# Expert matrices: output copies on ScalarE, another order of the low parts, raw weights as halves of their rows

## The chip, the cores and the metric

The kernel runs on one core of a Trainium2 chip. The metric is the device time of one execution in microseconds, as the median of several. The engines are TensorE (PE, its weight loads shown as PEld), VectorE (DVE), ScalarE (ACT), GpSimd (POOL) and SyncE (SP, which issues most transfers).

## The reference

One step of a two-layer diffusion backbone on 128 context tokens and 1024 latent tokens, width 1024, in float32. Layer 0 mixes tokens by a gated linear recurrence, layer 1 by a chunked spatial gate. Behind each mixer stands an expert-choice mixture of experts, which is where the change lies:

```
def _ec_moe(x, router, w_gate, w_up, w_down):
    cap = EC_FACTOR * (bsz * t) // N_EXPERTS        # 128 latent tokens, 16 context tokens per expert
    aff = jax.nn.softmax(xf @ router, axis=-1)
    g, idx = lax.top_k(aff.T, cap)
    xs = xf[idx]
    hh = silu(einsum('ecd,edf->ecf', xs, w_gate)) * einsum('ecd,edf->ecf', xs, w_up)
    out = einsum('ecf,efd->ecd', hh, w_down) * g[..., None]
    y = zeros_like(xf).at[idx.reshape(-1)].add(out.reshape(-1, d))
```

There are 16 experts in each of the two layers, each with three matrices of 1024x1024 float32, 4 MB each.

## The kernel before

**Numbers in two parts.** A float32 weight is scaled and written as the sum of two float16 numbers: `whi` (the rounded value, an ACT copy) and `wlo` (the rest, a DVE subtraction). The tokens are split likewise into `Sh` and `Sl`, the hidden activations into `Hh` and `Hl`. A product is three float16 matmuls: whi·Sh, whi·Sl, wlo·Sh.

**Steps.** An expert is worked off in 12 steps, which the code calls pairs, because each covers two blocks of 128 output columns. In step n, `i = n % 12`: i = 0 to 3 are the gate matrix, 4 to 7 the up matrix, 8 to 11 the down matrix. A step is 2 blocks x 8 slices of the inner dimension x 3 products = 48 matmuls of 128x144 (128 latent and 16 context tokens). They go into a tile `mm` of PSUM, one bank for each block, of which there are two, so that step n + 2 needs what step n left there to have been read. The program issues each step as 36 matmuls (inner slices 0 to 5), then other work, then the 12 matmuls of slices 6 and 7.

**What reads `mm` (`evacuate`, L1722 ff.).** Gate steps: ACT applies SiLU into `sg` (L1733). Up steps: DVE multiplies with `sg` into `t` (L1738); `hidden` then makes `Hh` (ACT, L1743; for the last of the four steps DVE, L1745) and `Hl` (DVE, L1746). Down steps: DVE writes the 128 latent columns into `oT` (L1752) and the 16 context columns into `pt` (L1753), each times a gain. Step 8 reads all of H, so `hidden` of step 7 stands right ahead of it.

**Around the steps.** An expert's tokens are gathered by an indirect transfer (`xg`), turned by 8 PE transposes in step 8 of the expert before (`xgT`, L1661), scaled by ACT into `tmp` (8 activations of 128x128, L1674) and split into `Sh` (ACT, L1685) and `Sl` (DVE, L1686), in two halves. A finished expert's `oT` is turned back by 8 transposes in step 1 of the next (`oTT`), scaled by ACT (`o`, L1765) and added to the result in DRAM by an indirect transfer.

**Weights ahead.** A raw half matrix of 2 MB (`raw`) is loaded by one transfer on SP (L1617) into one of five buffers: all 1024 rows, 512 of the 1024 columns, so 2 KB per row. `split_hi` and `split_lo` make the parts of a later step piece by piece, two pieces a step, each of 128 partitions x 1024 elements, into 12 buffers of `whi` and 12 of `wlo`. A piece is one block of 128 columns with all 8 inner slices. When the last piece of a raw half has its `wlo`, the buffer is given to the load of five halves later. Two tables, `HIS` and `LOS`, say for each of the 12 steps how many pieces are issued at three places: behind the 36 matmuls and ahead of `hidden`, behind `hidden`, and behind the last 12 matmuls. The high parts run about five steps ahead of the matmuls, the low parts four. The first four steps' pieces of a layer are loaded and split during the mixer by the class `First`.

Each engine works its queue strictly in order, so these tables decide what stands ahead of what on ACT and DVE:

```
            rest = evacuate(n - 1) if n > 0 else None
            if i == 8:
                rest()
                rest = None
            matmuls(n, range(6))
            ahead(n, 0)
            if rest:
                rest()
            ahead(n, 1)
```

**The last expert of layer 1** has the final norm beside its steps: ACT squares the finished rows, POOL multiplies them by the gain, DVE works out the factor 1/rms in small operations (L103 to L113).

Of the kernel before, what the change touches and what calls it, by code (L numbers as in the profile page):

```python
# [23 lines left out]
P = 128  # L24
KD = D // P
# [14 lines left out]
UP, DOWN = 2.0 ** 8, 2.0 ** -4  # L40
# [3 lines left out]
def tile_trunk(  # L44
# [10 lines left out]
    V, A, PE, G, SP = nc.vector, nc.scalar, nc.tensor, nc.gpsimd, nc.sync  # L55
# [34 lines left out]
    half = cp.tile([P, 1], F32, name="half")  # L90
# [140 lines left out]
    def rows(ch):  # L231
        return slice(ch * P, (ch + 1) * P)
# [147 lines left out]
    class First:  # L380


        N = 8

        def __init__(self, l, carry, room):
# [2 lines left out]

        def load(self, c):
            if c < self.N:  # L390
                self.raw[c] = self.room(f"first{self.l}_{c}").rearrange("p (k n) -> p k n", k=KD)
                SP.dma_start(self.raw[c], self.src[:, :, rows(c)])

        def split(self, c):
            if c < self.N:
                p = [self.carry.tile([P, KD, P], F16, tag=f"w{s}", name=f"w{s}{self.l}_f{c}", bufs=12) for s in ("hi", "lo")]
                split_up(self.raw.pop(c), *p)
                self.parts.append(p)

# [10 lines left out]
    class Route:  # L410
# [140 lines left out]
                A.activation(d[:, i], ps[:, P * i:P * (i + 1)], AF.Identity, bias=self.big[:, 1, 4 * q + i:4 * q + i + 1])  # L551

        def halve(self):
            self.xh, self.xl = (self.room(n, [P, KD, P], F32R) for n in ("xph", "xpl"))
            A.copy(self.xh, self.post.xnp.rearrange("t (k p) -> t k p", p=P))

        def halve_rest(self, h):
# [10 lines left out]
        def slots_prompt(self):  # L568

            pr = self.ps.tile([P, NE], F32, tag="misc", name=f"rank{self.l}", bufs=1)  # L570
            for e in range(NE):
                PE.matmul(pr[:, e:e + 1], self.gt[:, e], ones[:, 0:1], start=True, stop=True)
            rk = sm.tile([P, NE], F32, tag="rk", name=f"rk{self.l}")
            V.tensor_scalar_add(rk, pr, 1.0)
            self.oh = self.room("oh", [P, NE, CAPP], F32R)
            V.tensor_tensor(self.oh, rk[:, :, None].to_broadcast([P, NE, CAPP]),
                            slot1[:, None, 0:CAPP].to_broadcast([P, NE, CAPP]), op=OP.is_equal)

# [18 lines left out]
        def weights(self):  # L597

            self.og = self.room("og", [P, NE, CAPP], F32)
            V.tensor_tensor(self.og, self.oh.bitcast(F32), self.af[:, 8, :, None].to_broadcast([P, NE, CAPP]), op=OP.mult)  # L600
            self.ogT = self.ps.tile([P, 4, P], F32, tag="tr", name=f"ogT{self.l}")
            for h in range(2):
                PE.transpose(self.ogT[:, h], self.og[:, 8 * h:8 * h + 8].rearrange("p e s -> p (e s)"), ident)
# [991 lines left out]
    def moe(l, post, route, firsts, carry, close):  # L1595
        es = ExitStack()
        posm, info, pt, ohg, idxs, gs = route.posm, route.info, route.pt, route.ohg, route.idxs, route.gs
        wp = pool_of(es, f"moew{l}")
# [4 lines left out]
        g2 = cp.tile([P, 2, KD], F32, name=f"g2_{l}")  # L1603
        G.tensor_scalar(g2, modc[l, 5], 1.0 / (UP * DOWN), None, op0=OP.mult)

        raws, ws, xg, evac = {}, {}, {}, {}
        S, H, sg, oT, oTT, tmps = {}, {}, {}, {}, {}, {}
        NPAIR = 12 * NE

        def load(m):  # L1610

            if m >= 6 * NE:
                return
            e, which, half = m // 6, m % 6 // 2, m % 2
            t = raws[m] = wp.tile([P, KD, FF // 2], F32, tag="raw", name=f"raw{l}_{m}", bufs=5)
            w = (moe_w_gate, moe_w_up, moe_w_down)[which]
            SP.dma_start(t, w[l, e].rearrange("(k p) f -> p k f", p=P)[:, :, 512 * half:512 * (half + 1)])  # L1617

        def block(n, b):
            m, j = divmod(n, 2)  # L1620
            return raws[m][:, :, P * (2 * j + b):P * (2 * j + b + 1)]

        def split_hi(n, b):
            if n < NPAIR:
                hi = carry.tile([P, KD, P], F16, tag="whi", name=f"whi{l}_{n}_{b}", bufs=12)
                A.activation(hi, block(n, b), AF.Copy, scale=UP)  # L1626
                ws[n, b] = [hi]

        def split_lo(n, b):
            if n < NPAIR:  # L1630
                lo = carry.tile([P, KD, P], F16, tag="wlo", name=f"wlo{l}_{n}_{b}", bufs=12)
                V.scalar_tensor_tensor(lo, block(n, b), UP, ws[n, b][0], op0=OP.mult, op1=OP.subtract)  # L1632
                ws[n, b].append(lo)
                if n % 2 == 1 and b == 1:
                    raws.pop(n // 2)
                    load(n // 2 + 5)


        def slots_a(e):
# [24 lines left out]
        def tokens_b(e, ps, h):  # L1664

            if h == 0:
                tmps[e] = mp.tile([P, KD, 144], F32, tag="tmp", name=f"tmp{l}_{e}")
                V.tensor_copy(tmps[e][:, :, P:], pt[:, :, CAPP * e:CAPP * (e + 1)])
            for k in range(4 * h, 4 * h + 4):
                o = tmps[e][:, k, 0:P]  # L1670
                if e == 0 and h == 0:
                    V.tensor_scalar(o, ps[h][:, k], s2[:, 1, k:k + 1], sh2[:, 1, k:k + 1], op0=OP.mult, op1=OP.add)
                else:
                    A.activation(o, ps[h][:, k - 4 * h], AF.Identity, bias=sh2[:, 1, k:k + 1], scale=s2[:, 1, k:k + 1])  # L1674
# [14 lines left out]
        AHEAD = 4  # L1689
# [16 lines left out]
        tp = pool_of(es, f"moet{l}")  # L1706
        for h in range(2):
            tokens_c(0, h)
        split_hi(AHEAD, 0)


        def matmuls(n, ks):
            e, i = divmod(n, 12)
            hi, lo = S[e] if i < 8 else H[e]
            if n not in evac:
                evac[n] = psw.tile([P, 2, 512], F32, tag="mm", name=f"mm{l}_{n}", bufs=2)
            ps = evac[n]
            for b in range(2):
                wh, wl = ws[n, b]
                for k in ks:  # L1720
                    for i, (w, x) in enumerate(((wh, hi), (wh, lo), (wl, hi))):
                        PE.matmul(ps[:, b, 0:144], w[:, k], x[:, k], start=(k == 0 and i == 0), stop=(k == KD - 1 and i == 2))  # L1722

        def evacuate(n):
            e, i = divmod(n, 12)
            kind, j = divmod(i, 4)
            ps = evac.pop(n)
            js = slice(2 * j, 2 * j + 2)
            ps = ps[:, :, 0:144]
            if kind == 0:  # L1730
                if j == 0:
                    sg[e] = mp.tile([P, KD, 144], F32, tag="tmp", name=f"sg{l}_{e}")
                A.activation(sg[e][:, js], ps, AF.Silu, scale=1.0 / UP)  # L1733
            elif kind == 1:
                if j == 0:
                    H[e] = [tp.tile([P, KD, 144], F16, tag=f"H{x}", name=f"H{x}{l}_{e}") for x in "hl"]
                t = tp.tile([P, 2, 144], F32, tag="mmt", name=f"t{l}_{n}", bufs=2)
                V.scalar_tensor_tensor(t, ps, DOWN / UP, sg[e][:, js], op0=OP.mult, op1=OP.mult)  # L1738

                def hidden():  # L1740
                    hi, lo = (x[:, js] for x in H[e])
# [13 lines left out]

# [267 lines left out]
```

## Time and profile before

| | |
|---|---|
| median of 3 runs | 2587.98 us (2587.79 to 2589.66) |
| the profiled execution, its span | 2586.94 us, 2584.8 us |
| busy: PE, DVE, ACT, POOL | 2432.3 us (94%), 1909.0 (74%), 1641.5 (64%), 257.6 (10%) |
| mean granted PE clock | 0.974 |
| moved by the transfers | 647.19 MB, 250 GB/s in the mean |
| experts of layer 0; of layer 1 | about 569 to 1200 us; 1924 to 2562 us |

Busy time of an engine is a union of its instructions; neighbours may overlap by some tens of nanoseconds, so the distance from one start to the next is what an instruction costs its queue. "Idle before" is the time for which an engine stood still ahead of an instruction, with the one that released it. Matmuls are pipelined: one of 128x144 is listed with 226 ns, but the next starts much sooner.

### The profile page before, as it was taken

The page shows a single profiled execution, that of the slowest core. Times are in us where ns is not written, and L with a number is a line of the kernel's source. Part 1 is how long each engine was busy: PE and PEld are TensorE (multiplying, and loading weights), DVE is VectorE, ACT ScalarE, POOL GpSimd, SP SyncE. Part 2 cuts the span into 40 slices and gives each one's busy share as a digit, 9 for nine tenths or more (in the row PEclk, how much of TensorE's full clock was granted, in tenths as well). Part 3 has the DMA queues.
Part 4 walks back from the last instruction along what each step waited for, and adds up shares of the span by engine and source line. Part 5 has one row for each costly group of instructions (what it writes and reads, how often), then busy time and mean ns, then how long its engine had stood idle before and what let it go on. Part 6 is the DMA issues. An engine that isn't in the chain of part 4 may idle for free. (4 is left out here: it accounts for less than half of the span.)

```text
span 2584.8 us, 60548 instructions
## 1 busy us (share of the span) xinstructions
PE 2432.3 (94%) x26054; PEld 1850.6 (72%) x26054; DVE 1909.0 (74%) x2790; ACT 1641.5 (64%) x2336; POOL 257.6 (10%) x307
## 2 busy tenths in 40 slices
PE   6999989969999999998999999999969999999996
PEld 4455554459999999997434455534459999999995
DVE  6888895479999999996622333445679999999997
ACT  5877883448777777885623333434448778777874
POOL 1011101100000000001201100100100000000003
PEclk9999999979999999998999999999979999999998
DMA  9466216459999999994544533457559999999994
GB/s 321 166 206 206 76 64 200 157 205 339 342 355 354 345 330 360 342 354 136 178 151 163 175 114 111 153 190 233 191 212 342 346 350 355 347 329 360 341 350 164
DMA packets 330236, 647.19 MB, mean 250 GB/s; under 512 B 15555, under 2 KB 69367, under 8 KB 329967
## 3 DMA queue, kind: packets, MB, share of 16 engines
q1 hardware_dynamic: 306352, 568.49, 62.0%
q0 software_dynamic: 21136, 74.67, 9.2%
q8 instruction: 204, 3.34, 0.5%
q10 hardware_dynamic: 2478, 0.16, 0.1%
q14 instruction: 66, 0.53, 0.1%
HBM read 576.59 MB, written 66.68 MB: 249 GB/s over the span
## 5 line engine op out<-in xcount | busy, mean ns | idle before, releaser
L1722 PEld LDWEIGHTS <-whi 128*128 128x128 f16 x12032 | 966.8, 98 | 28.0 <-issue 22.2
L1632 DVE SCALAR_TENSOR_TENSOR wlo<-raw,whi 128x1024 f16<-128x1024 f32 x752 | 885.5, 1221 | 25.5 <-ACT whi L1626 25.5
L1626 ACT ACTIVATE whi<-raw 128x1024 f16<-128x1024 f32 x752 | 756.0, 1060 | 53.3 <-PE mm L1722 49.8
L1722 PE MATMUL mm<-Sh,whi 128*128 128x144 f16 x3968 | 747.6, 226 | 0.8 <-DVE t L1738 0.8
L1722 PE MATMUL mm<-Sh,wlo 128*128 128x144 f16 x3968 | 747.6, 226 | 0.0
L1722 PE MATMUL mm<-Sl,whi 128*128 128x144 f16 x3968 | 747.6, 226 | 0.0
L1722 PEld LDWEIGHTS <-wlo 128*128 128x128 f16 x6016 | 589.2, 98 | 13.9 <-issue 13.7
L1722 PE MATMUL mm<-Hh,whi 128*128 128x144 f16 x2048 | 390.2, 227 | 20.3 <-DVE Hh L1745 15.4
L1722 PE MATMUL mm<-Hl,whi 128*128 128x144 f16 x2048 | 389.1, 227 | 9.8 <-DVE Hl L1746 9.8
L1722 PE MATMUL mm<-Hh,wlo 128*128 128x144 f16 x2048 | 389.1, 227 | 0.0
L1327 PE MATMUL uv<-sgw,h_hi 128*128 128x512 f16 x576 | 219.6, 381 | 0.0
L1328 PE MATMUL uv<-sgw,h_hi 128*128 128x512 f16 x576 | 219.3, 381 | 0.0
L1329 PE MATMUL uv<-sgw,h_lo 128*128 128x512 f16 x576 | 219.1, 380 | 0.0
L1333 ACT ACTIVATE uvo<-uv 128x512 f32<-128x512 f32 x72 | 43.0, 597 | 198.5 <-PE uv L1329 198.5
L896 PE MATMUL pj<-hn_hi,wh 128*128 128x386 f16 x480 | 157.8, 329 | 1.9 <-ACT hn_hi L116 1.9
L897 PE MATMUL pj<-hn_lo,wh 128*128 128x386 f16 x480 | 157.5, 328 | 0.2
L898 PE MATMUL pj<-hn_hi,wl 128*128 128x386 f16 x480 | 157.5, 328 | 0.0
L1766 POOL DMA_INDIRECT x_d<-o,idx x31 | 55.8, 1799 | 965.1 <-ACT o L1765 933.8
L1440 DVE SCALAR_TENSOR_TENSOR uvo<-sv,bs,uvo 128x256 f32<-128x256 f32 x72 | 31.5, 480 | 140.4 <-PE sv L1437 140.4
L1346 DVE TENSOR_TENSOR uvo<-uvo,gain 128x512 f32<-128x512 f32 x36 | 24.9, 691 | 134.1 <-ACT uv L1345 134.1
L1674 ACT ACTIVATE tmp<-xgT,modc,ns 128x128 f32<-128x128 f32 x248 | 90.5, 468 | 45.2 <-DVE t L1738 40.2
L1327 PEld LDWEIGHTS <-h_hi 128*128 128x128 f16 x576 | 56.5, 98 | 69.4 <-issue 10.1
(413 smaller groups left out, 3892.0 us busy)
## 6 DMA issues: line engine op xcount, KB each, us to landing
raw<-in_moe_w_up_dram SPq DMA_DIRECT2D x64, 2048.0 KB
raw<-in_moe_w_down_dram SPq DMA_DIRECT2D x64, 2048.0 KB
raw<-in_moe_w_gate_dram SPq DMA_DIRECT2D x60, 2048.0 KB
wm<-in_w_mod_dram SPq DMA_DIRECT2D x96, 512.0 KB
m<-mt_d SPq DMA_DIRECT2D x72, 256.0 KB
sgr<-in_sg_w_in_dram SPq DMA_DIRECT2D x32, 512.0 KB
win<-in_lru_w_in_dram SPq DMA_DIRECT2D x20, 512.0 KB
v_d<-uvo POOLq DMA_DIRECT2D x36, 256.0 KB, 2.4
```

Of the source, the lines that this page charges most:

```text
L896: PE.matmul(ps[:, i, 0:WP], wh[:, k], hi[k][:, cs], start=(k == 0), stop=False)
L897: PE.matmul(ps[:, i, 0:WP], wh[:, k], lo[k][:, cs], start=False, stop=False)
L898: PE.matmul(ps[:, i, 0:WP], wl[:, k], hi[k][:, cs], start=False, stop=(k == KD - 1))
L1327: PE.matmul(ps, hi[:, k, cs], th[:, k % 4], start=(k == 0), stop=False)
L1328: PE.matmul(ps, hi[:, k, cs], tl[:, k % 4], start=False, stop=False)
L1329: PE.matmul(ps, lo[:, k, cs], th[:, k % 4], start=False, stop=(k == KD - 1))
L1333: A.activation(o, ps, AF.Gelu_apprx_tanh, scale=1.0 / UP)
L1626: A.activation(hi, block(n, b), AF.Copy, scale=UP)
L1632: V.scalar_tensor_tensor(lo, block(n, b), UP, ws[n, b][0], op0=OP.mult, op1=OP.subtract)
L1674: A.activation(o, ps[h][:, k - 4 * h], AF.Identity, bias=sh2[:, 1, k:k + 1], scale=s2[:, 1, k:k + 1])
L1722: PE.matmul(ps[:, b, 0:144], w[:, k], x[:, k], start=(k == 0 and i == 0), stop=(k == KD - 1 and i == 2))
L1766: G.indirect_dma_start(out=x_d[0:NS, :], out_offset=bass.IndirectOffsetOnAxis(ap=idxs[:, e:e + 1], axis=0), in_=o, in_offset=None, compute ...
```

## The change

1. **Outputs.** `oT` of a down step is written by ACT in two activations of 128x128 (a copy with a factor per partition) instead of one DVE product of 128x256. DVE keeps `pt`. The copy of `pt` into `tmp` goes from DVE to ACT as well, but for a layer's first expert.
2. **Order of the parts.** New `HIS` and `LOS`, 24 pieces per expert as before. In steps 5 to 7 one low part stands ahead of `hidden`, and in step 7 it is the only one. The second half of the tokens' scaling moves from step 9 to step 10, its split from 10 to 11. Two high parts instead of one are issued ahead of the loop.
3. **Raw weights as halves of their rows.** A raw half is now 512 of the 1024 rows with all columns, 4 KB per row, and a piece is 4 inner slices of both blocks (128 x 4 x 256). Each step takes one piece from each of two raw halves, so a pair of halves serves four steps and the two are given up one right after the other. `First` loads and splits the same way (1 KB instead of 512 B per row).
4. **Buffers.** 14 of `whi` and 13 of `wlo`. `xph`, `xpl` and `oh` of the routing stage become float16, so that its 16 matmuls of 128x256 per layer are float16 with weight loads of their own.

DVE in expert 6 of layer 0 before, from `t` of step 6 (`t_78`) to the first reads of a down step; `sg`, `Hh`, `Hl`, `raw` as above, `waits` names the engine or transfer queue waited for:

```order
L1738 SCALAR_TENSOR_TENSOR t_78_10399<-mm_78_10338,sg_6_9999 128x288 [waits PE_49]
L1746 TENSOR_TENSOR Hl_6_10274<-t_78_10399,Hh_6_10273 128x288 [waits Activation_49]
L1632 SCALAR_TENSOR_TENSOR wlo_84_0_10442<-raw_42_9936,whi_84_0_10393 128x1024 [waits DMAHW0_49]
L1632 SCALAR_TENSOR_TENSOR wlo_84_1_10458<-raw_42_9936,whi_84_1_10438 128x1024
L1738 SCALAR_TENSOR_TENSOR t_79_10460<-mm_79_10401,sg_6_9999 128x288 [waits PE_49]
L1745 CAST Hh_6_10273<-t_79_10460 128x288 [waits DVE_49]
L1746 TENSOR_TENSOR Hl_6_10274<-t_79_10460,Hh_6_10273 128x288 [waits DVE_49]
L1632 SCALAR_TENSOR_TENSOR wlo_85_0_10503<-raw_42_9936,whi_85_0_10456 128x1024 [waits Activation_49]
L1668 COPY tmp_7_10526<-pt_4674 128x8x16
L1752 TENSOR_TENSOR oT_6_10532<-mm_80_10464,g_0_4845 128x256 [waits PE_49]
```

The same place in the changed kernel:

```order
L1742 SCALAR_TENSOR_TENSOR t_78_10425<-mm_78_10362,sg_6_10023 128x288 [waits PE_49]
L1634 SCALAR_TENSOR_TENSOR wlo_84_0_10466<-raw_42_9961,whi_84_0_10399 128x1024 [waits DMAHW0_49]
L1750 TENSOR_TENSOR Hl_6_10298<-t_78_10425,Hh_6_10297 128x288 [waits Activation_49]
L1742 SCALAR_TENSOR_TENSOR t_79_10484<-mm_79_10427,sg_6_10023 128x288 [waits PE_49]
L1749 CAST Hh_6_10297<-t_79_10484 128x288 [waits DVE_49]
L1750 TENSOR_TENSOR Hl_6_10298<-t_79_10484,Hh_6_10297 128x288 [waits DVE_49]
L1634 SCALAR_TENSOR_TENSOR wlo_84_1_10527<-raw_43_10156,whi_84_1_10423 128x1024 [waits DMAHW1_49]
L1634 SCALAR_TENSOR_TENSOR wlo_85_0_10552<-raw_42_9961,whi_85_0_10464 128x1024
L1759 TENSOR_TENSOR pt_4674<-mm_80_10488,g_0_4845 128x2x16 [waits PE_49,Activation_49]
```

Of the two low parts that stood between `Hl` of step 6 and `t_79` of step 7 one stands ahead of that `Hl` and the other behind the three operations of step 7. `oT` is gone from DVE, and `pt` waits for Activation.

ACT in the same expert before, from the last high part of step 7 through steps 8 to 11:

```order
L1626 ACTIVATE whi_85_1_10501<-raw_42_9936 128x1024 [waits PE_49,Activation_49]
L1674 ACTIVATE tmp_7_10526<-xgT_7_10505,modc_3_1390,ns_2_3377 128x128 [waits DVE_49,PE_49,Activation_49]
L1674 ACTIVATE tmp_7_10526<-xgT_7_10505,modc_3_1390,ns_2_3377 128x128 x7
L1626 ACTIVATE whi_86_0_10588<-raw_43_10044 128x1024 [waits DMAHW1_49,PE_49]
L1685 CAST Sh_7_10594<-tmp_7_10526 128x576 [waits DVE_49,Activation_49]
L1626 ACTIVATE whi_86_1_10637<-raw_43_10044 128x1024 [waits PE_49]
L1685 CAST Sh_7_10594<-tmp_7_10526 128x576 [waits Activation_49]
L1626 ACTIVATE whi_87_0_10655<-raw_43_10044 128x1024 [waits PE_49]
L1626 ACTIVATE whi_87_1_10698<-raw_43_10044 128x1024 [waits PE_49]
```

ACT in the changed kernel, from the first output copy, ahead of which four `tmp` stand, to the second `Sh`:

```order
L1758 ACTIVATE oT_6_10560<-mm_80_10488,g_0_4845 128x128 [waits PE_49]
L1758 ACTIVATE oT_6_10560<-mm_80_10488,g_0_4845 128x128
L1628 ACTIVATE whi_87_0_10601<-raw_42_9961 128x1024
L1628 ACTIVATE whi_87_1_10617<-raw_43_10156 128x1024
L1688 CAST Sh_7_10621<-tmp_7_10554 128x576 [waits Activation_49]
L1758 ACTIVATE oT_6_10560<-mm_81_10564,g_0_4845 128x128 [waits PE_49]
L1758 ACTIVATE oT_6_10560<-mm_81_10564,g_0_4845 128x128
L1677 ACTIVATE tmp_7_10554<-xgT_7_10529,modc_3_1390,ns_2_3377 128x128 x4
L1628 ACTIVATE whi_88_0_10683<-raw_44_10202 128x1024 [waits DMAHW2_49]
L1758 ACTIVATE oT_6_10560<-mm_82_10628,g_0_4845 128x128 [waits PE_49]
L1758 ACTIVATE oT_6_10560<-mm_82_10628,g_0_4845 128x128
L1688 CAST Sh_7_10621<-tmp_7_10554 128x576 [waits Activation_49]
```

The eight `tmp` and the two `Sh` are drawn apart, and three of an expert's four pairs of `oT` copies stand ahead of the second `Sh`; the fourth follows it after one high part.

The diff, without the float16 lines of the routing stage, whose tiles `xph`, `xpl`, `oh` only change their type, and with one row pair of each table:

```
         def load(self, c):                                   # class First
             if c < self.N:
-                self.raw[c] = self.room(f"first{self.l}_{c}").rearrange("p (k n) -> p k n", k=KD)
-                SP.dma_start(self.raw[c], self.src[:, :, rows(c)])
+                n, h = divmod(c, 2)
+                self.raw[c] = self.room(f"first{self.l}_{c}").rearrange("p (k n) -> p k n", k=4)
+                SP.dma_start(self.raw[c], self.src[:, 4 * h:4 * h + 4, 256 * n:256 * (n + 1)])
...
-            t = raws[m] = wp.tile([P, KD, FF // 2], F32, tag="raw", name=f"raw{l}_{m}", bufs=5)
+            t = raws[m] = wp.tile([P, KD // 2, FF], F32, tag="raw", name=f"raw{l}_{m}", bufs=5)
...
-            SP.dma_start(t, w[l, e].rearrange("(k p) f -> p k f", p=P)[:, :, 512 * half:512 * (half + 1)])
+            SP.dma_start(t, w[l, e].rearrange("(k p) f -> p k f", p=P)[:, 4 * half:4 * half + 4])
-        def block(n, b):
-            m, j = divmod(n, 2)
-            return raws[m][:, :, P * (2 * j + b):P * (2 * j + b + 1)]
+        def block(n, h):
+            return raws[n // 4 * 2 + h][:, :, 256 * (n % 4):256 * (n % 4 + 1)]
...
-                if n % 2 == 1 and b == 1:
-                    raws.pop(n // 2)
-                    load(n // 2 + 5)
+                if n % 4 == 3:
+                    m = n // 4 * 2 + h
+                    raws.pop(m)
+                    load(m + 5)
...
-                V.tensor_copy(tmps[e][:, :, P:], pt[:, :, CAPP * e:CAPP * (e + 1)])
+                (A.copy if e else V.tensor_copy)(tmps[e][:, :, P:], pt[:, :, CAPP * e:CAPP * (e + 1)])
...
-        split_hi(AHEAD, 0)
+        for h in range(2):
+            split_hi(AHEAD, h)
...
             for b in range(2):
-                wh, wl = ws[n, b]
                 for k in ks:
+                    wh, wl = (w[:, k % 4, P * b:P * (b + 1)] for w in ws[n, k // 4])
...
-                V.tensor_tensor(oT[e][:, js], ps[:, :, 0:P], g2[:, 1, js, None].to_broadcast([P, 2, P]), op=OP.mult)
+                for b in range(2):
+                    c = 2 * j + b
+                    A.activation(oT[e][:, c], ps[:, b, 0:P], AF.Copy, scale=g2[:, 1, c:c + 1])
...
-        LOS = ((1, 0, 1), (2, 0, 1), (1, 0, 1), (1, 0, 1), (2, 0, 1), (0, 1, 1), (0, 1, 1), (0, 1, 1), (1, 0, 0), (0, 0, 1), (1, 0, 1), (1, 0, 1))
+        LOS = ((1, 0, 1), (2, 0, 1), (1, 0, 1), (1, 0, 1), (2, 0, 1), (1, 1, 0), (1, 1, 0), (1, 0, 0), (1, 0, 1), (1, 0, 1), (1, 0, 1), (0, 0, 1))
...
-            if more and i == 9:
+            if more and i == 10:
                 tokens_b(e + 1, hold["x"], 1)
-            if more and i == 10:
+            if more and i == 11:
                 tokens_c(e + 1, 1)
```

## Rows read from the trace of the kernel before

**Rows 1.** Windows, layer 0, an expert of layer 1: PE, PEld, DVE, ACT, POOL

```profile
590.00:1165.00 575.00, 562.37 (x8784) 556.84 (x8782) 524.64 (x710) 455.35 (x619) 43.65 (x28) 1.00 0.97 346
...
2037.21:2076.28 39.07, 38.28 (x604) 37.97 (x602) 35.68 (x48) 31.09 (x43) 3.14 (x2) 1.00 0.99 352
```

**Rows 2.** Waits, whole run, layer 0, layer 1: us, times, longest

```profile
PE mm L1722 <- DVE Hh L1745: 15.4, 30, 0.5
...
PE mm L1722 <- DVE Hl L1746: 4.1, 15, 0.3
PE mm L1722 <- DVE t L1738: 0.9, 2, 0.4
...
PE mm L1722 <- DVE Hl L1746: 5.7, 16, 1.7
```

**Rows 3.** Timelines, PE and DVE, at step 8: start, us, instruction, [idle before]

```profile
2031.83 1.04 PE L1661 MATMUL xgT<-ident,xg 128*128 128x128 f32 x8
2033.38 0.22 PE L1722 MATMUL mm<-Hh,whi 128*128 128x144 f16 x1 [0.51 <-DVE Hh L1745]
...
2030.26 2.35 DVE L1632 SCALAR_TENSOR_TENSOR wlo<-raw,whi 128x1024 f16<-128x1024 f32 x2
2032.53 0.45 DVE L1738 SCALAR_TENSOR_TENSOR t<-mm,sg 128x288 f32<-128x288 f32 x1
2033.01 0.31 DVE L1745 CAST Hh<-t 128x288 f16<-128x288 f32 x1
2033.36 0.46 DVE L1746 TENSOR_TENSOR Hl<-t,Hh 128x288 f16<-128x288 f32 x1
```

**Rows 4.** Chain behind that wait: start, us, what

```profile
2033.87 15.10 PE mm L1722 x239
```

**Rows 5.** Groups by line, three experts: count | busy, mean ns | idle

```profile
L1674 ACT ACTIVATE tmp<-xgT,modc,ns 128x128 f32<-128x128 f32 x24 | 8.7, 468 | 4.0 <-DVE t L1738 4.0
...
L1752 DVE TENSOR_TENSOR oT<-mm,g 128x256 f32<-128x256 f32 x12 | 5.0, 419 | 0.0
L1686 DVE TENSOR_TENSOR Sl<-tmp,Sh 128x576 f16<-128x576 f32 x6 | 4.5, 755 | 2.7 <-ACT Sh L1685 2.7
```

**Rows 6.** Timeline of ACT, steps 8 and 9 of that expert

```profile
2033.10 2.91 ACT L1674 ACTIVATE tmp<-xgT,modc,ns 128x128 f32<-128x128 f32 x8 [1.34 <-DVE t L1738]
2035.87 1.09 ACT L1626 ACTIVATE whi<-raw 128x1024 f16<-128x1024 f32 x1
2036.82 0.70 ACT L1685 CAST Sh<-tmp 128x576 f16<-128x576 f32 x1
```

**Rows 7.** DMA, 40 slices of 2030-2050, 1880-1916, 2530-2546; one issue

```profile
GB/s 418 422 397 401 414 418 406 401 401 430 406 401 401 430 365 254 205 295 307 348 406 414 410 410 406 414 393 205 82 0 20 106 160 385 426 406 389 401 426 406
...
GB/s 0 0 46 182 400 405 412 412 403 410 410 412 407 410 405 414 410 410 405 414 407 405 412 410 394 400 407 412 414 410 391 378 57 16 0 0 0 0 0 0
...
GB/s 10 0 0 0 164 20 61 430 399 440 420 410 420 410 420 399 451 410 440 410 451 389 389 410 399 430 430 420 400 420 440 410 430 430 225 20 31 31 0 0
...
2044.40 0.37 SPq L1617 DMA_DIRECT2D raw<-in_moe_w_gate_dram  x1
```

**Rows 8.** Timelines of DVE, ACT, POOL and PE, last expert of layer 1

```profile
2542.37 2.57 DVE L1746 TENSOR_TENSOR Hl<-t,Hh 128x288 f16<-128x288 f32 x1
...
2548.42 2.33 DVE L111 TENSOR_TENSOR rstf<-rsrf 128x4 f32<-128x4 f32 x1 [1.23 <-POOL rsrf L105]
...
2541.03 1.05 ACT L1833 ACTIVATE fin<-fin 128x1024 f32<-128x1024 f32 x1
2542.21 1.06 ACT L1833 ACTIVATE fin<-fin 128x1024 f32<-128x1024 f32 x1
...
2542.26 4.90 POOL L1840 TENSOR_TENSOR fin<-fin,gain 128x1024 f32<-128x1024 f32 x2 [9.75 <-ACT fin L1833]
...
2548.37 9.27 POOL L1840 TENSOR_TENSOR fin<-fin,gain 128x1024 f32<-128x1024 f32 x4
...
2555.84 0.30 PE L1722 MATMUL mm<-Hh,whi 128*128 128x144 f16 x1 [4.00 <-DVE pt L1753]
```

More of the change, by code (lines that the diff above doesn't have):

```diff
@@ L390, in load @@
             if c < self.N:
-                self.raw[c] = self.room(f"first{self.l}_{c}").rearrange("p (k n) -> p k n", k=KD)
-                SP.dma_start(self.raw[c], self.src[:, :, rows(c)])
+                n, h = divmod(c, 2)
+                self.raw[c] = self.room(f"first{self.l}_{c}").rearrange("p (k n) -> p k n", k=4)
+                SP.dma_start(self.raw[c], self.src[:, 4 * h:4 * h + 4, 256 * n:256 * (n + 1)])
         def split(self, c):
             if c < self.N:
-                p = [self.carry.tile([P, KD, P], F16, tag=f"w{s}", name=f"w{s}{self.l}_f{c}", bufs=12) for s in ("hi", "lo")]
+                p = [self.carry.tile([P, 4, 256], F16, tag=f"w{s}", name=f"w{s}{self.l}_f{c}", bufs=dict(hi=14, lo=13)[s]) for s in ("hi", "lo")]
                 split_up(self.raw.pop(c), *p)
@@ L553, in halve @@
         def halve(self):
-            self.xh, self.xl = (self.room(n, [P, KD, P], F32R) for n in ("xph", "xpl"))
+            self.xh, self.xl = (self.room(n, [P, KD, P], F16) for n in ("xph", "xpl"))
             A.copy(self.xh, self.post.xnp.rearrange("t (k p) -> t k p", p=P))
@@ L574, in slots_prompt @@
             V.tensor_scalar_add(rk, pr, 1.0)
-            self.oh = self.room("oh", [P, NE, CAPP], F32R)
+            self.oh = self.room("oh", [P, NE, CAPP], F16)
             V.tensor_tensor(self.oh, rk[:, :, None].to_broadcast([P, NE, CAPP]),
@@ L599, in weights @@
             self.og = self.room("og", [P, NE, CAPP], F32)
-            V.tensor_tensor(self.og, self.oh.bitcast(F32), self.af[:, 8, :, None].to_broadcast([P, NE, CAPP]), op=OP.mult)
+            V.tensor_tensor(self.og, self.oh, self.af[:, 8, :, None].to_broadcast([P, NE, CAPP]), op=OP.mult)
             self.ogT = self.ps.tile([P, 4, P], F32, tag="tr", name=f"ogT{self.l}")
@@ L1614, in load, with split_hi, split_lo @@
             e, which, half = m // 6, m % 6 // 2, m % 2
-            t = raws[m] = wp.tile([P, KD, FF // 2], F32, tag="raw", name=f"raw{l}_{m}", bufs=5)
+            t = raws[m] = wp.tile([P, KD // 2, FF], F32, tag="raw", name=f"raw{l}_{m}", bufs=5)
             w = (moe_w_gate, moe_w_up, moe_w_down)[which]
-            SP.dma_start(t, w[l, e].rearrange("(k p) f -> p k f", p=P)[:, :, 512 * half:512 * (half + 1)])
-        def block(n, b):
-            m, j = divmod(n, 2)
-            return raws[m][:, :, P * (2 * j + b):P * (2 * j + b + 1)]
-        def split_hi(n, b):
+            SP.dma_start(t, w[l, e].rearrange("(k p) f -> p k f", p=P)[:, 4 * half:4 * half + 4])
+        def block(n, h):
+            return raws[n // 4 * 2 + h][:, :, 256 * (n % 4):256 * (n % 4 + 1)]
+        def split_hi(n, h):
             if n < NPAIR:
[L1625 to L1629, printed above, removed]
+                hi = carry.tile([P, 4, 256], F16, tag="whi", name=f"whi{l}_{n}_{h}", bufs=14)
+                A.activation(hi, block(n, h), AF.Copy, scale=UP)
+                ws[n, h] = [hi]
+        def split_lo(n, h):
             if n < NPAIR:
-                lo = carry.tile([P, KD, P], F16, tag="wlo", name=f"wlo{l}_{n}_{b}", bufs=12)
-                V.scalar_tensor_tensor(lo, block(n, b), UP, ws[n, b][0], op0=OP.mult, op1=OP.subtract)
-                ws[n, b].append(lo)
-                if n % 2 == 1 and b == 1:
-                    raws.pop(n // 2)
-                    load(n // 2 + 5)
+                lo = carry.tile([P, 4, 256], F16, tag="wlo", name=f"wlo{l}_{n}_{h}", bufs=13)
+                V.scalar_tensor_tensor(lo, block(n, h), UP, ws[n, h][0], op0=OP.mult, op1=OP.subtract)
+                ws[n, h].append(lo)
+                if n % 4 == 3:
+                    m = n // 4 * 2 + h
+                    raws.pop(m)
+                    load(m + 5)
         def slots_a(e):
@@ L1718, in matmuls @@
             for b in range(2):
-                wh, wl = ws[n, b]
                 for k in ks:
+                    wh, wl = (w[:, k % 4, P * b:P * (b + 1)] for w in ws[n, k // 4])
                     for i, (w, x) in enumerate(((wh, hi), (wh, lo), (wl, hi))):
-                        PE.matmul(ps[:, b, 0:144], w[:, k], x[:, k], start=(k == 0 and i == 0), stop=(k == KD - 1 and i == 2))
+                        PE.matmul(ps[:, b, 0:144], w, x[:, k], start=(k == 0 and i == 0), stop=(k == KD - 1 and i == 2))
         def evacuate(n):
@@ L1893, in moe @@
         hold = {}
-        his = iter([(m, b) for m in range(AHEAD, NPAIR + 1) for b in range(2)][1:])
+        his = iter([(m, b) for m in range(AHEAD + 1, NPAIR + 1) for b in range(2)])
         los = iter([(m, b) for m in range(AHEAD, NPAIR) for b in range(2)])
@@ L1902, in ahead @@
                 split_lo(m, b)
-        HIS = ((2, 0, 1), (1, 0, 1), (1, 0, 1), (1, 0, 1), (2, 0, 1), (1, 0, 1), (1, 0, 1), (1, 0, 1), (1, 0, 0), (0, 0, 1), (1, 0, 1), (1, 0, 1))
-        LOS = ((1, 0, 1), (2, 0, 1), (1, 0, 1), (1, 0, 1), (2, 0, 1), (0, 1, 1), (0, 1, 1), (0, 1, 1), (1, 0, 0), (0, 0, 1), (1, 0, 1), (1, 0, 1))
+        HIS = ((1, 0, 1), (1, 0, 1), (2, 0, 1), (1, 0, 2), (1, 0, 1), (1, 0, 1), (1, 0, 1), (1, 0, 1), (1, 0, 1), (1, 0, 1), (0, 0, 1), (0, 0, 1))
+        LOS = ((1, 0, 1), (2, 0, 1), (1, 0, 1), (1, 0, 1), (2, 0, 1), (1, 1, 0), (1, 1, 0), (1, 0, 0), (1, 0, 1), (1, 0, 1), (1, 0, 1), (0, 0, 1))
         for n in range(NPAIR):
```

## The prediction

> **What bounds the kernel now.** I looked first at the windows by stage. In the experts PE is busy 562 of 575 us at full granted clock, and a middle expert takes 39.07 us, 38.28 of them PE, 35.68 DVE, 31.09 ACT [rows 1]. So the expert stages, 1250 of 2585 us (32 experts at 39.07), are PE's own pace plus a little waiting, and the change can win at most that waiting. The waits of PE come next: 30 times 0.51 us for `Hh` and 30 times about 0.27 us for `Hl` [rows 2], once per expert, always in step 8. Nowhere in the experts does PE wait for a transfer or for ACT in the steady state.
>
> The timelines show how this wait arises [rows 3]. PE has finished the 36 matmuls of step 8 that it can do, turns the next tokens (until 2032.87), and then stands until 2033.38, because DVE spent 2030.26 to 2032.5 on two low parts and began `t` of step 7 at 2032.53. Behind the wait the matmuls follow each other every (15.10 - 0.23)/238 = 62.5 ns [rows 4], so a step is 48 x 62.5 = 3.0 us. Step 7 therefore ended about 2032.87 - 1.04 - 36 x 0.0625 = 2029.6, and `t` was 2.9 us late behind queued work, not for want of data.
>
> **The change part by part.**
>
> *Low parts in another order.* In step 7 one low part stands ahead of the last `Hl` and none between it and `t` of step 7. From the end of step 6 DVE now has `t` (0.45), one low part (2.35/2 = 1.18), `Hl` (0.46), together 2.1 us inside a step of 3.0, so `t` of step 7 can start as soon as its matmuls are through (their 0.23 us). From there `Hh` starts 0.48 later, `Hl` 0.35 after that and takes 0.46: 1.5 us after the end of step 7 all of H is there. PE needs it after 2.25 + 1.04 = 3.3 us. Even a DVE that is 1.2 us late from the steps before still makes it. The wait goes: 15.4 + 4.1 + (5.7 - 1.7) = 23.5 us, where the 1.7 is the longest one, in the very last expert, which has another cause (below). What was hidden there, the displaced low parts, moves to steps 8 to 10, where `oT` no longer takes DVE 4 x 0.42 = 1.7 us per expert [rows 5]. DVE falls from 35.7 to about 34.0 us.
>
> *Outputs on ACT.* Not seen before; nearest is `tmp`, also ACT from PSUM, 128x128, with one operand more. It costs (2035.87 - 2033.10)/8 = 0.346 us from start to start, 0.468 alone [rows 5, 6]. I take 0.346, because the copies come in twos and between other ACT work; an even cheaper one would change nothing, since it is hidden. Eight are 2.8 us per expert, 31.1 + 2.8 + 0.3 (the small copy of `pt`) = 34.2 of 38.3 us. The tight place is the second `Sh`, now behind three pairs of copies. From the end of step 8: 0.23 for the matmuls, six copies 2.08, three high parts at 0.95 2.85, four `tmp` 1.38, two `Sh` at 0.70 1.40, together 7.94; `Sl` (0.76 and a little) is done at 8.8. PE reads this half after three steps and 12 matmuls, 9.75 us. The margin of 1.0 us holds for copies up to 0.346 + 1.0/6 = 0.51 us, above the 0.468 of a lone one. So I cost this edit at nothing.
>
> The Trainium skill speaks against the move: "ScalarE: Activation LUTs", Rules for kernel authors, gives multiplications to VectorE, which it calls faster per element. The row agrees in size (0.69 us on ACT against 0.42 on DVE); by the rule the move loses 1.1 us of engine time per expert, by the row of PE's waits none of it is on the path.
>
> *`pt` behind `oT`.* `pt` on DVE now waits for both ACT copies of its step, which the order shows as a wait for Activation. Queued behind it are low parts and `Sl`. It adds at most 0.23 + 0.69 + 0.12 = 1.04 us four times, less where DVE comes late itself. 34.0 + 4 x 1.04 = 38.2, just inside the 38.3 that PE needs. The low parts run four steps ahead, so single waits are absorbed: nothing, with little to spare.
>
> *Raw halves of rows.* PE waits for no transfer, so a faster one gains nothing; the question is a loss. An expert moves 39.07 x 0.352 = 13.7 MB. Rows of 2 KB run at about 408 GB/s in the long stretch of the second line of [rows 7], rows of 4 KB (the final norm's loads) at about 417 in the third. The first line has one gap per expert: six slices of 0.5 us that move 573 in place of 6 x 410, 2.3 us lost. Shortening the expert by 0.78 leaves 1.5. A load takes about 7 us from its issue: the one at 2044.40 is at full rate in the slice from 2046.0, and 2 MB at 410 are 5.1. The tightest of the new halves is given up late in step 2 and first read late in step 6, 12 us later; 7 and 2.6 for an expert's gather and scatter (1.05 MB) leave 2.4. Cost nothing. The strides of the raw halves are the only other difference for ACT and DVE, and PE's weights stay rows of 128 in a row.
>
> *Float16 routing tiles, three more buffers, one high part more ahead of the loop.* Matmuls of the same columns; the 16 new weight loads per layer hide as those of 128x144 do at 62.5 ns. If none hid, at most 16 x 0.15, my allowance, on layer 0's entry: 0 to +2.4, taken 0.
>
> *The ends.* Layer 0's last step: the second ACT copy ends 0.346 + 0.468 = 0.8 behind its start against 0.42, so +0.4. Layer 1's last expert: POOL's gain products block small DVE work; `Hl` took 2.57 us and a 128x4 operation 2.33, one POOL product (9.27/4) [rows 8]. `pt` of step 9 stands behind three such, and PE waited 4.00 for it. Squares 1 to 3 now stand behind the output copies of step 8, which wait for that step, while before ACT squared from 2541.03 on every 1.18 us. Measured from the end of step 6: step 8 ends at about 6.5, copies 0.7, three squares 3.5, the factor's first steps 1.5, three blocked operations 7.0, `pt` 0.2, so PE goes on at about 19.4. Before, step 6 ended at 2544.94 (the end of `Hl`) - 1.7 - 2.25 - 3.0 = 2538.0, and PE went on at 2555.84, 17.8 later. That is +1.6, and +0.4 for the last copies. The 1.7 us wait for `Hl` shrinks inside this sum. Bounds: -1.7 if the squares do not matter, +5 if two more POOL products get in front.
>
> The expert that carries the prompt products has two further waits for `t` per layer (0.9 in layer 0 [rows 2]); its queue is as full as before, so I leave them: 0, bounds -1.7 and +1.
>
> Sum: -23.5 + 0.4 + 2.0 = -21.1 us on an execution of 2586.94 (span 2584.8). The median, 2587.98, stands 1.0 above that, and I take it as base: **2566.9 us**.
>
> **Rivals.**
>
> *A. ACT too late for the next tokens.* Lone durations throughout give 0.23 + 6 x 0.468 + 3 x 1.09 + 4 x 0.468 + 1.40 + 0.8 = 10.4 against 9.75: a new wait of 0.65 in step 0 and a gain of 0.13 x 30 = 4, less 2.4 at the ends, 2586. Half of that wait gives 2576; I put 2581. For it: ACT is the engine that gains work, in strict order. Against: its rows overlap by 0.1 us wherever two stand together.
>
> *B. DVE held by `pt`, slower.* If the copies often stand behind a high part (0.95), `pt` waits 1.5 us on average: 34.0 + 6.0 = 40.0 us per expert, +0.93 x 30 + 2.4, 2618. It decides from a mean wait of 1.07 us (PE starts to wait), and loses from 1.27 on. For it: DVE's 34.0 leave little. Against: ACT reaches step 8 idle, and where ACT is late DVE has low parts of its own in front.
>
> *C. Transfers bind.* The DMA share is 0.99, and if 351 GB/s is what they can do, the expert stays at 39.07 and the ends cost: 2590, no change. Against: stretches above 400 and the gap. The Trainium skill ("DMA: Bandwidth & Descriptors", Where 436 GB/s comes from) has a rule that speaks for C: from HBM to SBUF the HBM side, about 358 GB/s, binds. By it 13.7 MB take 38.4 us, the gain stops at 30 x 0.67 = 20 less 2.4, and the time is 2570; the stretch at 408 disagrees, and I follow the row.
>
> **How the numbers follow.** Forecast 0.74, own range 2561 (all lower bounds) to 2574 (the upper bounds of ends and weight loads); A 0.10, B 0.10, C 0.06. Under 0.2% (5 us) this kernel can't be told from no change. Faster: 0.74 and most of A, 0.80; same: rest of A and C, 0.10; slower: B, 0.10. The range 2559 to 2585 takes the forecast and nearly all of A; B and most of C stay out.
>
> **What would show it.** Right: no PE wait for `Hh` or `Hl` in step 8, an expert at 38.3 us, ACT busy near 34, DVE near 34 with a new wait of `pt` for ACT of 2 to 3 us per expert, output copies near 0.47 us listed. Layer 1's last expert somewhat longer than before. Wrong: PE waiting for `Sl` in step 0 (A), for `pt` in steps 10 and 11 or a `wlo` anywhere (B), ACT waiting for `raw` (C).

## The result and the profile after

| | before | changed |
|---|---|---|
| median, same chip | 2588.07 us | 2553.89 us (2553.10 to 2557.19) |
| ratio, 95% interval | | 0.9872 (0.9860 to 0.9883) |
| profiled span | 2584.8 us | 2551.0 us |

Faster, as forecast, but by 34 us where 21 were forecast; the time lies below the range. I read the windows first: layer 0, then an expert of layer 1 from its first `xgT` transpose to that of the next. The columns are us, then busy time (and count) of PE, PEld, DVE, ACT, POOL, then PE clock, DMA share, GB/s.

```profile
590.00:1165.00 575.00, 574.51 (x9058) 573.58 (x9055) 520.69 (x651) 494.96 (x770) 42.34 (x29) 1.00 0.94 353
...
2012.92:2050.87 37.95, 37.95 (x603) 37.93 (x602) 34.38 (x44) 32.96 (x51) 2.93 (x2) 1.00 0.95 361
```

An expert takes 37.95 us, not the 38.3 forecast: 1.12 less than before, though only 0.79 stood idle beside the PE column there [rows 1]. The neighbouring column had the right number: PEld was busy 37.97 of 39.07 us, so 1.10 stood still. The waits of TensorE for tiles in the changed kernel, whole run:

```profile
PE mm L1726 <- DVE pt L1759: 6.6, 1, 6.6
...
PE mm L1726 <- DVE Hl L1750: 1.0, 2, 0.5
```

The 30 waits for `Hh` and nearly all of those for `Hl` [rows 2] are gone. PE and DVE at the same place as in [rows 3]:

```profile
2012.88 1.04 PE L1664 MATMUL xgT<-ident,xg 128*128 128x128 f32 x8
2013.75 0.23 PE L1726 MATMUL mm<-Hh,whi 128*128 128x144 f16 x1
...
2010.06 0.46 DVE L1750 TENSOR_TENSOR Hl<-t,Hh 128x288 f16<-128x288 f32 x1
2010.83 0.46 DVE L1742 SCALAR_TENSOR_TENSOR t<-mm,sg 128x288 f32<-128x288 f32 x1 [0.31 <-PE mm L1726]
2011.32 0.31 DVE L1749 CAST Hh<-t 128x288 f16<-128x288 f32 x1
2011.66 0.46 DVE L1750 TENSOR_TENSOR Hl<-t,Hh 128x288 f16<-128x288 f32 x1
2012.04 2.35 DVE L1634 SCALAR_TENSOR_TENSOR wlo<-raw,whi 128x1024 f16<-128x1024 f32 x2
```

DVE now waits for PE ahead of `t`, all of H is there at 2012.12, and PE asks for it at 2013.75. These two PE rows also give the true size of the old wait. Without a wait the first matmul starts 2013.75 - 2012.88 = 0.87 us after the first transpose; before it was 2033.38 - 2031.83 = 1.55 [rows 3], so 0.68 was lost, where the row says 0.51. The next matmul followed at 2033.87 [rows 4], 0.49 later instead of 0.0625: 0.43 lost, where the waits list 0.27. Together 1.11. The listed idle is counted from the modelled end of the matmul ahead, 0.23 us after its start, though the next can start after 0.0625. PEld's waits in layer 0 before said it too, 17.1 us in a window with 15 of these waits ("issue": it waited for nothing that the profile shows):

```profile
PEld L1722 <- issue: 17.1, 32, 0.7
```

### The profile page after: what moved, and what is told of

Read it like the earlier page. It is cut to its first block, busy times and chain, and to the rows that moved or that the text cites. A ratio compares the mean times of both kernels' runs of the same rounds, so it can differ in the third digit from the quotient of the medians.

```text
span 2551.0 us, 60657 instructions
## 1 busy us (share of the span) xinstructions
PE 2420.1 (95%) x26054; PEld 1847.2 (72%) x26054; DVE 1865.2 (73%) x2632; ACT 1698.0 (67%) x2622; POOL 251.0 (10%) x307
## 5 line engine op out<-in xcount | busy, mean ns | idle before, releaser
L1772 POOL DMA_INDIRECT x_d<-o,idx x31 | 49.8, 1606 | 930.7 <-ACT o L1771 870.5
L1758 ACT ACTIVATE oT<-mm,g 128x128 f32<-128x128 f32 x256 | 83.3, 394 | 36.3 <-PE mm L1726 36.3
```

Of the source, the lines that this page charges most:

```text
L1758: A.activation(oT[e][:, c], ps[:, b, 0:P], AF.Copy, scale=g2[:, 1, c:c + 1])
L1772: G.indirect_dma_start(out=x_d[0:NS, :], out_offset=bass.IndirectOffsetOnAxis(ap=idxs[:, e:e + 1], axis=0), in_=o, in_offset=None, compute ...
```

## Experiments

Theory T: the order of the low parts carries the whole gain, and the wait is worth 1.1 us per expert. Rivals: R1, the listed 0.78 is all that the order gives, and the larger rows of the transfers bring the rest; R2, VectorE had to be relieved of the outputs. Each ratio is against the kernel before on the same chip. The time of an expert is the distance from its first matmul to that of the next.

**1. The order alone, on the kernel before.**

```
-LOS = (..., (0, 1, 1), (0, 1, 1), (0, 1, 1), (1, 0, 0), (0, 0, 1), (1, 0, 1), (1, 0, 1))   # steps 5 to 11
+LOS = (..., (1, 1, 0), (1, 1, 0), (1, 0, 0), (1, 0, 1), (0, 0, 1), (1, 0, 1), (1, 0, 1))
```

> The kernel before with the low parts alone in another order: in steps 5 to 7 one stands ahead of `hidden`, in step 7 it is the only one, and the displaced one goes to step 8. Outputs stay on VectorE, raw halves and pieces stay by columns, 12 buffers of each part. Theory T (the whole gain is the wait for H in step 8, and it is worth not the 0.78 us per expert that the idle rows list but 1.07, counted from start to start): about 2588 - 30 x 1.07 - 1 for the prompt experts = 2555, between 2551 and 2559, a middle expert at 38.0 us. Rival R1 (the order brings only the listed 0.78 per expert, the rest comes from the transfers with rows of 4 KB): 2564 or more, an expert at 38.3. Rival R2 (VectorE must first be relieved of the output copies): over 2575, with a new wait of TensorE for a low part or for `pt`.

2549.5 us, ratio 0.9851 (0.9836 to 0.9866), an expert at 37.95. That is 1.5 us under T's range: in its profile the first expert of layer 0 also took 38.10 us where it was 41.29 before (on that at the end), and the last one of layer 1 44.30 where it was 45.49. The window of layer 0:

```profile
590.00:1165.00 575.00, 574.52 (x9057) 573.59 (x9055) 536.41 (x725) 465.27 (x637) 128.16 (x29) 1.00 0.99 351
```

PEld is busy 573.6 of 575 us, as in the changed kernel, with the outputs on DVE (536 us busy), rows of 2 KB and 12 buffers of each part. Four entries of one table give the whole gain.

**2. One low part moved.** Step 7 `(0, 1, 1)` to `(0, 1, 0)`, step 8 `(1, 0, 0)` to `(1, 0, 1)`, nothing else.

> The kernel before with one low part alone moved: the one behind `hidden` of step 7's place goes to the end of step 8, steps 5 and 6 stay. By T most of the wait goes, since one of the two parts between `Hl` of step 6 and `t` of step 7 is gone: an expert 38.1 to 38.2, the prompt expert still with part of its waits, 2555 to 2563. If both parts must go, because VectorE then still reaches `t` too late: 38.5 or more, over 2568.

2553.64, ratio 0.9868 (0.9852 to 0.9885), an ordinary expert at 37.96, the prompt expert at 41.56 (42.67 before, 40.92 changed). One part out of the way is enough for the ordinary experts; my 38.1 to 38.2 and 2555 to 2563 were too careful.

**3. The old order in the changed kernel.**

> The changed kernel with the table of the low parts as before, all else as changed. T (the order alone carries the gain): the wait for H in step 8 is back, an expert at about 38.9 us, 2554 + 30 x 0.9 = 2580 to 2588. R1 and R2 (transfers or relief carry 8 to 13 us of the gain, the order 23): 2574 to 2578.

2585.77, ratio 0.9999 (0.9990 to 1.0008): all else of the change, without the order, is worth nothing in sum. The window of layer 0:

```profile
590.00:1165.00 575.00, 565.51 (x8832) 559.96 (x8830) 508.42 (x638) 487.95 (x755) 41.23 (x28) 1.00 0.92 348
```

and its waits there:

```profile
PE mm L1726 <- DVE Hh L1749: 4.6, 15, 0.5
PE mm L1726 <- DVE Hl L1750: 4.1, 15, 0.3
```

The wait is back, though a little shorter: 0.31 us listed for `Hh` instead of 0.51, and most experts take 38.81 us instead of 39.07. So the rest of the change does relieve the old order somewhat, by some 5 us over all experts; which part of it does was not tried. The last expert (47.44 us, 45.49 before) and the stretches between the experts of the two layers take it back. R1 and R2 had the total at 2574 to 2578.

**4. Outputs back on VectorE, in the changed kernel** (`oT` as one DVE product, `pt` copied into `tmp` by DVE).

> The changed kernel with the outputs `oT` and the small copy of `pt` into `tmp` back on VectorE. T (the move of the outputs only makes room that is not needed): 2554 (2550 to 2559), an expert at 38.0 us, VectorE at about 35.7 per expert. R2 (the relief carries part of the gain): 2562 or more, with TensorE waiting for `Hh`, `Hl`, a low part or `Sl`.

2551.89, ratio 0.9867 (0.9852 to 0.9882), an expert at 37.95 with DVE busy 539.7 of 575 us in layer 0. R2 falls.

**5. Outputs on ScalarE, on the kernel before**, the reverse edit.

> The kernel before with the outputs `oT` and the small copy of `pt` on ScalarE, and nothing else. T (the wait for H stands in the order of VectorE's queue in step 7, which this does not touch): 2587 to 2591, an expert at 39.07 us. R2 (relief of VectorE by 1.7 us per expert takes part of the wait away): 2565 to 2582, an expert under 38.9.

2591.97, ratio 1.0020 (1.0010 to 1.0029): slower, 1 us over T's range, an expert at 39.11. Layer 0 and the last expert of layer 1:

```profile
PE mm L1722 <- DVE Hh L1745: 7.7, 15, 0.5
...
PE mm L1722 <- DVE pt L1755: 6.6, 1, 6.6
```

The wait for `Hh` is the same 15 times 0.5, though DVE is busy for 504.2 us of this window instead of 524.6; that for `pt` near the end grows from 4.0 [rows 8] to 6.6.

**6. Columns instead of halves of rows, in the changed kernel.**

> The changed kernel with raw halves and pieces by columns as before (rows of 2 KB, in the class First 512 bytes), all else as changed. T: 2554 (2550 to 2558), an expert at 38.0 us, since TensorE waits for no transfer. R1 (rows of 4 KB give the part of the gain that I did not forecast, 13 us): 2562 to 2568.

2555.81, ratio 0.9881 (0.9865 to 0.9896), an expert at 37.95. R1 falls: no matmul waits for the transfer of a weight either way, and the 1.9 us to the changed kernel lie within the intervals.

**7. Twelve buffers of each part, in the changed kernel.**

> The changed kernel with 12 buffers of each part instead of 14 and 13, all else as changed. T2 (with pieces that span both blocks of a step a part's buffer comes free only with the step's last matmuls, so that the room for the next parts is the tight thing and the buffers are needed): ACT waits for TensorE ahead of its high parts, an expert 1 to 2 us longer, 2554 + 30 x 1.6 = 2602 (2580 to 2615). Rival (the parts run four steps ahead, 8 pieces, so 12 buffers do): 2554 (2550 to 2558), an expert at 37.95.

2583.53, ratio 0.9987 (0.9978 to 0.9996), an expert at 38.93. Waits in layer 0:

```profile
ACT whi L1628 <- PE mm L1726: 54.7, 69, 2.1
DVE pt L1759 <- ACT oT L1758: 49.4, 30, 3.0
...
PE mm L1726 <- DVE pt L1759: 7.2, 15, 0.5
```

ACT stands still ahead of a high part whose buffer PE still reads; the output copies queue behind it, `pt` behind those, and PE waits for `mm`. So the move of the outputs put `pt` behind ACT's whole queue, and the buffers keep that from mattering. T2 was right on the wait and too high on its price.

**8. The same with columns.** T2 blamed the shape of the pieces, so this run takes the other shape.

> The changed kernel with raw halves and pieces by columns as before and 12 buffers of each part. It tells why the buffers are needed. T2 as I put it for the run with 12 buffers (pieces that span both blocks come free too late): with pieces by columns 12 do, an expert at 37.95, 2554 (2550 to 2559). Rival T3 (it is the new table of the high parts, which runs up to one piece further ahead, whatever the shape of a piece): the wait stays, an expert near 38.7 to 38.95, 2576 to 2584.

2628.47, ratio 1.0163 (1.0146 to 1.0180), an expert at 40.41: worse, against both numbers. Layer 0:

```profile
DVE pt L1758 <- ACT oT L1757: 53.8, 28, 3.6
ACT whi L1628 <- PE mm L1725: 49.5, 56, 2.5
...
PE mm L1725 <- DVE pt L1758: 14.5, 14, 1.0
...
PE mm L1725 <- ACT Hh L1746: 3.9, 14, 0.3
PE mm L1725 <- DVE Hl L1749: 3.8, 14, 0.3
```

PE waits for `pt` and again for H, this time for an `Hh` that ACT makes. So the shape is not to blame in the way T2 had it; pieces by halves of rows cost less here when buffers are short. The program suggests why, but no run tries it apart: the last 12 matmuls of a step (slices 6 and 7 of both blocks) read both pieces when they are columns, and only the second when they are halves of rows, so by halves the first buffer comes free 12 matmuls earlier. What needs the extra buffers is then among the rest of the change: the new table of the high parts, the outputs on ACT, the later scaling of the tokens. Which of these it takes was not tried either. The diff ahead leaves the table of the high parts out:

```
-HIS = ((2, 0, 1), (1, 0, 1), (1, 0, 1), (1, 0, 1), (2, 0, 1), (1, 0, 1), (1, 0, 1), (1, 0, 1), (1, 0, 0), (0, 0, 1), (1, 0, 1), (1, 0, 1))
+HIS = ((1, 0, 1), (1, 0, 1), (2, 0, 1), (1, 0, 2), (1, 0, 1), (1, 0, 1), (1, 0, 1), (1, 0, 1), (1, 0, 1), (1, 0, 1), (0, 0, 1), (0, 0, 1))
```

**9. Another end of layer 1, in the changed kernel**, and **10. the same end on the kernel of experiment 1.** The edit, shortened (the lines of the steps without their `lambda`, what stands behind step 11 as a comment):

```
-st[8] = [squares(0)]
-st[9] = [squares(1, 2, 3), gains(0, 1), rstd(0)]
-st[10] = [squares(4, 5), gains(2), scale(V, 0)]
-st[11] = [squares(6, 7), gains(3), scale(V, 1)]
+st[8] = [squares(0, 1, 2, 3)]
+st[9] = [squares(4, 5), rstd(0), norm(0)]      # norm: factor and gain in one DVE operation
+st[10] = [squares(6, 7), norm(1), norm(2)]
+st[11] = [rstd(1), norm(3)]                    # norm(4) to norm(7) behind part(0), part(1)
```

> The changed kernel with another end of layer 1: the gain products leave GpSimd (VectorE multiplies by factor and gain in one operation), the squares of rows 0 to 3 stand ahead of step 8's output copies, the factor's small operations and all eight normed rows are spread over steps 9 to 11 and the end. The same is computed. If TensorE's 6.6 us wait for `pt` in step 11 comes from VectorE's small operations that GpSimd's gain products hold up: that wait is gone, the last matmul is some 8 us earlier, and 2554 becomes 2543 (2538 to 2548). If it comes from ScalarE alone (squares ahead of the output copies): the wait stays at 3 us or more, 2549 to 2555.

> The kernel before with the low parts in another order, as in the run of that alone, and the other end of layer 1. If the order of the low parts is the whole gain and the end is a matter of GpSimd's products: 2549.5 less the 3.3 us wait for `pt`, about 1 us of half clock and some 4 us of row scaling behind the last matmul, 2541 (2537 to 2546), the fastest of all. If the end hangs on the transfers of the rows: 2547 or more.

2544.71, ratio 0.9832 (0.9818 to 0.9845), and 2544.68, ratio 0.9836 (0.9823 to 0.9850): both are faster than the kernel before and the changed kernel, and the two can't be told apart, where I had expected the second to be the fastest. The changed kernel near the end, DVE, then POOL and PE:

```profile
2514.01 0.17 DVE L103 TENSOR_SCALAR rsvf<-fss 128x4 f32<-128x4 f32 x1 [3.21 <-ACT fin L1839]
2515.41 2.31 DVE L111 TENSOR_TENSOR rstf<-rsrf 128x4 f32<-128x4 f32 x1 [1.22 <-POOL rsrf L105]
2517.75 2.27 DVE L112 SCALAR_TENSOR_TENSOR rstf<-rstf,rsvf 128x4 f32<-128x4 f32 x1
2520.06 2.26 DVE L113 SCALAR_TENSOR_TENSOR frstd<-rstf,rsrf 128x4 f32<-128x4 f32 x1
2522.25 0.18 DVE L1759 TENSOR_TENSOR pt<-mm,g 128x32 f32<-128x32 f32 x1
...
2515.36 9.25 POOL L1846 TENSOR_TENSOR fin<-fin,gain 128x1024 f32<-128x1024 f32 x4
...
2522.48 0.28 PE L1726 MATMUL mm<-Hh,whi 128*128 128x144 f16 x1 [6.56 <-DVE pt L1759]
```

The same operations in experiment 9, with no product on POOL:

```profile
2514.89 0.16 DVE L111 TENSOR_TENSOR rstf<-rsrf 128x4 f32<-128x4 f32 x1 [1.23 <-POOL rsrf L105]
2515.09 0.16 DVE L112 SCALAR_TENSOR_TENSOR rstf<-rstf,rsvf 128x4 f32<-128x4 f32 x1
2515.28 0.16 DVE L113 SCALAR_TENSOR_TENSOR frstd<-rstf,rsrf 128x4 f32<-128x4 f32 x1
```

Each takes 0.16 us instead of 2.3. The run changes two things at once: counted from the expert's first matmul the three begin at 30.2 us instead of 33.5, because the squares stand earlier, and they last 0.55 us in all instead of 6.9, which is the larger part. PE no longer waits, and from its first to its last matmul of the steps this expert takes 36.81 us in both experiments, 46.06 in the changed kernel and 44.30 in experiment 1. What follows the start of the last of them is 23.9 us in experiment 10 (23.1 in experiment 1), where I had expected some 4 less. DVE and PE there:

```profile
2526.84 3.67 DVE L1857 SCALAR_TENSOR_TENSOR fin<-fin,frstd,gain 128x1024 f32<-128x1024 f32 x3
...
2532.20 1.21 DVE L1798 TENSOR_TENSOR x<-x,yp 128x1024 f32<-128x1024 f32 x1
...
2525.55 3.25 PE L1797 MATMUL yp<-pd 128*128 128x512 f32 x6 [3.40 <-ACT pd L116]
```

`yp` is there at 2528.8, but three normed rows and the last expert's rows stand ahead of the addition that needs it, until 2532.2: the work was moved out of one wait into another.

## Why the forecast was too small

**What bounds the kernel** failed in one clause: "the change can win at most that waiting", by which I meant 39.07 - 38.28. The 62.5 ns from matmul to matmul were right, the unused time was not. The Trainium skill ("Perfetto Trace Analysis", Identifying the Most-Contended Engine) says that matmul busy time is no good measure of the distance to the roof, because matmuls are pipelined, and names the busy share of the weight loads as one of two better ones. This case agrees: by PEld the forecast is 1.10 x 30 = 33 us of waiting, and it was 33.5.

The terms beside what they measured, read from the start of each expert's first matmul in the two profiles:

| term | forecast | measured |
|---|---|---|
| 30 waits in step 8 | -23.5 | -33.5 (1.118 each) |
| two prompt experts, beyond that | 0 | -1.3 (42.67 to 40.92 each) |
| layer 1's last expert and behind it | +2.0 | +0.3 (45.49 to 46.06, then -0.3) |
| all else | +0.4 | +0.7 |
| sum | -21.1 | -33.8 (2584.8 to 2551.0) |

*Low parts in another order.* The mechanism was right: experiments 1 to 3 give and take the gain with this table alone. The term was mis-sized: I added up the idle time as listed (0.78 us per expert) and did not compare starts (1.118). 10.0 of the 12.7 us missing are here.

*Outputs on ACT, cost nothing*: right in the experts (experiment 4). The copies were cheaper than the 0.47 us I expected to see listed, and ACT takes 32.96 us per expert, not 34.2:

```profile
L1758 ACT ACTIVATE oT<-mm,g 128x128 f32<-128x128 f32 x112 | 36.6, 396 | 5.3 <-PE mm L1726 5.3
```

But the argument for hiding them was incomplete: it holds with 14 and 13 buffers and not with 12 (experiment 7), and I had put the buffers among the edits that cost nothing. Rival A did not occur. My verdict on the rule of the Trainium skill ("ScalarE: Activation LUTs", Rules for kernel authors), that the move costs engine time but nothing on the path, holds for the steady state, where ACT has 1.9 us more per expert and DVE 1.3 less; in the last expert the move costs PE 2.6 us more wait (experiment 5). The rule's reason is a figure for bf16, while these copies are float32.

*`pt` behind `oT`*: the wait appeared, smaller than the 2 to 3 us expected, 27.5/15 = 1.8 us per expert, and PE does not feel it. DVE is at 34.38, forecast 34.0. Rival B did not occur here, but experiments 7 and 8 are that rival: `pt` waits 3.3 to 3.8 us per expert there, and PE then waits for `pt`.

```profile
DVE pt L1759 <- ACT oT L1758: 27.5, 30, 1.6
```

*Raw halves, cost nothing*: right (experiment 6). Rival C falls: the expert moves 361 GB/s in 37.95 us, and the row at 408 that I followed was the better guide. By the rule of the Trainium skill ("DMA: Bandwidth & Descriptors", Where 436 GB/s comes from) the expert would have stopped at 38.4.

*Float16 routing tiles.* The 0.15 us for a weight load that does not hide, my upper bound, rests on no row, and no run has these tiles alone; experiment 3 has them with all else but the order, at nothing in sum.

*The ends.* The squares behind the output copies made PE's wait for `pt` 6.6 us in place of 4.0. From the end of step 6 to the matmul behind that wait I had 19.4 us against 17.8 and it was 18.7 against 18.0: the 1.7 us wait for `Hl` just before vanished altogether, where my sum had kept some 0.5 of it. With a last step 0.2 us shorter the expert is 0.6 us longer. *The prompt experts* I left as they were because "its queue is as full as before"; the same order relieved them of 0.6 us each.

## What to carry to other kernels

Size a wait of a pipelined engine by the distance between starts, with and without the wait, or by its weight loads; idle listed behind a modelled end falls short, here by 30%. When an edit comes as a bundle, run its smallest part alone first: here one moved instruction per expert carried the gain (experiment 2), and the rest added nothing to it. Small operations at an end that queue behind products on GpSimd can cost TensorE more than their own length: three of 0.16 us took 6.9 us here, and TensorE stood for 6.6.

## What the hardware showed unexpectedly

A 128x4 operation on DVE took 2.3 us beside a POOL product and 0.16 without, while `pt`, which reads PSUM, took 0.18 once it was at the head of the queue, beside the same products. The Trainium skill ("GPSIMD Engine Reference", 8. Key points) has the two engines share their interfaces to SBUF, with contention for DVE operations that have two SBUF inputs or run in a 2-port performance mode. The three operations have two inputs and agree. A longer one in the changed kernel reads one tensor beside a factor per partition, and it too took longer while the last product (until 2524.61) ran; no run shows its mode:

```profile
2522.36 2.80 DVE L1854 TENSOR_SCALAR fin<-fin,frstd 128x1024 f32<-128x1024 f32 x1
...
2525.18 0.74 DVE L1854 TENSOR_SCALAR fin<-fin,frstd 128x1024 f32<-128x1024 f32 x1
```

After PE's 6.6 us standstill the 48 matmuls of step 11 took 5.5 us instead of 3.0. The window of the changed kernel, where the granted clock (third from the right) was 0.53, mostly the lower level of 1.2 GHz:

```profile
2522.40:2528.10 5.70, 5.62 (x50) 5.62 (x50) 3.52 (x4) 0.00 (x0) 2.21 (x1) 0.53 0.38 153
```

The kernel before shows the same behind its 4.00 us (5.6 us, clock 0.51), so this is no part of the difference between the two. In experiment 9 PE doesn't stand still, and the granted clock is 1.00, the level of 2.4 GHz, to the last step, which takes 3.0 us. The clock at layer 0's entry differed too; the same 5 us in the changed kernel

```profile
570.00:575.00 5.00, 5.00 (x44) 5.00 (x43) 4.80 (x5) 3.48 (x4) 0.00 (x0) 0.50 0.01 3
```

and in experiment 1:

```profile
570.00:575.00 5.00, 3.06 (x40) 2.57 (x40) 4.44 (x9) 4.44 (x8) 0.00 (x0) 1.00 0.00 0
```

The first expert takes 40.59 us in the one profile and 38.10 in the other, most of the 2.7 us between their spans. Executions of one kernel differ as much: the four of experiment 4 run from 2549.07 us at a mean granted clock of 0.975 to 2554.45 at 0.972. Whether the kernels differ in this as well was not settled.
